# Weights of three head groups and of the last stage prepared block by block in the second layer, with their subtractions on VectorE

## The chip, the core and the metric

The kernel runs on one core of a Trainium2 chip. Its engines are TensorE (PE: matmuls, and weight loads, PEld), VectorE (DVE), ScalarE (ACT), GpSimd (POOL) and SyncE (SP), which issues most DMAs; 16 DMA engines carry these. The metric is the device time of one execution in microseconds; lower is better. Before the change it was 2925.16 us, the median of 3 runs (2920.04 to 2928.3).

## What is computed

One inference step of a two-layer hybrid decoder, on a prompt of 2048 positions and 8 samples of 4 positions, with a model width of 1024. Cut to its core:

```python
def gla_mixer(h, state0, norm_g, w_in, w_gate2, b_gate, out_norm_g, w_out):   # layer 0
    u = rmsnorm(h, norm_g)
    proj = u @ w_in
    q, k, v, gate, g_low = jnp.split(proj, ...)
    log_a = jax.nn.log_sigmoid((g_low @ w_gate2 + b_gate).astype(jnp.float32)) / A_GATE_NORMALIZER
    o, state = gla_recurrence(...)                 # 4 heads, a 128 x 512 state each
    o = rmsnorm(o, out_norm_g).reshape(bsz, seq_len, BRANCH_WIDTH).astype(h.dtype)
    return (o * jax.nn.silu(gate)) @ w_out, state

k, v = shared_kv(h, kv_norm, w_k, w_v, k_norm, pos)                           # once, after layer 0

q, gate = jnp.split(rmsnorm(h, norm_g) @ w_in, [BRANCH_WIDTH], axis=-1)       # layer 1
q = rope(rmsnorm(q.reshape(bsz, seq_len, B_HEADS, B_HEAD_DIM), q_norm_g), pos)
o = swa_banded(q, k, v, sinks)                     # 128 positions back, 32 query heads on 4 key heads
return (o.reshape(bsz, seq_len, BRANCH_WIDTH) * jax.nn.silu(gate)) @ w_out
```

## The kernel before

Every float32 operand of a matmul is split in two float16 tiles, a high and a low half (`split`: ScalarE writes the high half, VectorE the low one from it), and a product is three matmuls (`PASSES`). A weight must be split too. Weights of the second layer are split ahead of time by *preparations*: a load into `wraw` (3 buffers) on SP's queue, a `split` into `pst` (2 buffers), and a store on GpSimd's queue to memory, from which a later stage fetches the finished halves. There are two kinds:

- `Unit.prepare`: the weights of the second layer's projections, half a unit (128 x 512) at a time. Each of the 4 head groups (`gw[0]` to `gw[3]`) has 16 halves for `q` and the gate; group 0 has 8 more for keys and values.
- `form_steps`: the factors of the two output projections, which are computed with 7 products in place of 8. For each of 8 row blocks it forms 7 tiles of 128 x 512 from four quarters of the weight (`put`), three of them straight and four after a subtraction each (`sub`, on GpSimd). `wfa` is the first layer's output weight, `wfd` the second layer's.

Stages, with their time in the profile: the **first layer** (36 to 1195 us) runs over 4 heads, and in each over 4 *quarters* of the prompt (512 positions, `blocks`), with the next quarter's scores (`level_steps`) woven into this one's projections. In quarters 0, 1 and 2 `some(PR[j])` hands out preparations, 4, 8 and 7 of them at each of three places, at a lower priority (`behind(..., 200)`), so that they run later than they are written. The list has 192: 8 of the rope tables, 56 for `wfa`, 72 for the groups, 56 for `wfd`. Quarter 3 holds the samples' work, and quarters 2 and 3 also convert the next head's own weights into `W`. Then the **first output projection** (to about 1595 us).

The **second layer** (1595 to about 2600 us) runs over 64 *blocks*: 4 head groups times 16 chunks of 128 positions. The loop over `t` has three blocks in flight (n = t + 3): the matmuls of block n's projections (`f` in `ORDER`), the scores of block n - 2 (`A`) and the values of block n - 3 (`B`). `pin` holds TensorE to that written order. Scores go over VectorE (maximum), ScalarE (exponential, `o` and `lev`, L1432) and a `split` to `v`, from which SP's queue transposes them to `sth` and `pst` (L1438) for the values. `q` passes through `qT`, `kT`, `qe` and a transpose to `X` (L1389); keys and values go to memory as `Kd` and `Vd` and come back into `gl` and `rmask`. The next group's prepared weights are fetched in the group's 13th block. Last comes the second output projection (from about 2600 us), with `wfd` fetched from block 50 on.

The order on each engine is fixed when the program is built: a scheduler places instructions by priority, and an engine then runs them strictly in that order. Each DMA on SP's queue is also in order with all others there.

## Time and profile before

| | |
|---|---|
| median of 3 runs | 2925.16 us (2920.04 to 2928.3) |
| the profiled execution's own time | 2933.08 us |
| its span, first to last instruction | 2931.3 us |
| granted TensorE clock, mean | 0.974 |
| busy: matmuls, VectorE, ScalarE, GpSimd | 93%, 69%, 51%, 41% |

The profile is of one execution. It has instructions with their times, the idle time ahead of each and what ended it ("waits"), and busy times of any stretch. Names such as `pst<-wraw` are the program's tiles, output first; L197 is a line of the program. SPq and POOLq are the queues on which SP and GpSimd issue DMAs.

### The profile page before, as it was taken

Reading aid. Unit: us, or ns where it says so; the run is one execution under the profiler, and the core shown is the slowest. Engines: PE = TensorE matmul, PEld = TensorE weight load, DVE = VectorE, ACT = ScalarE, POOL = GpSimd, SP = SyncE. Lnnn points to the kernel's source line nnn. Section 1 sums busy time; section 2 is a strip of 40 time slices with the busy share of each in tenths; the row PEclk is TensorE's granted clock in tenths of the full one; section 3 lists DMA queues with packets and bytes.
Section 4 is the critical chain, followed back from the end, with each engine's and each line's share of the span. In section 5 each row is a group of like instructions: output and inputs, shape, how many; then the busy total and the mean of one; then the engine's idle time right before and its main releaser. Section 6 shows DMA issues by size and latency. Waiting matters only on the chain.

```text
span 2931.3 us, 52081 instructions
## 1 busy us (share of the span) xinstructions
PE 2727.8 (93%) x18942; PEld 1380.9 (47%) x18942; DVE 2034.1 (69%) x4055; ACT 1489.3 (51%) x3481; POOL 1199.9 (41%) x1591
## 2 busy tenths in 40 slices
PE   6889999899989989999998999999999999988999
PEld 3444544344434444444543555555555555543444
DVE  6778779778777888567572575677767766776653
ACT  6665666566556655433231555566666656651110
POOL 2254235422432355312123686566557656530000
PEclk9999999999999999999999999999999999999999
DMA  8353224453563354886559555867777778798651
GB/s 215 81 142 104 88 101 140 149 161 119 173 193 109 122 171 159 230 189 154 118 147 237 112 118 124 202 111 132 165 127 129 139 153 165 154 226 178 131 112 55
DMA packets 786202, 427.46 MB, mean 146 GB/s; under 512 B 630928, under 2 KB 700504, under 8 KB 785912
## 3 DMA queue, kind: packets, MB, share of 16 engines
q1 hardware_dynamic: 768504, 373.72, 55.7%
q0 software_dynamic: 15360, 50.34, 4.5%
q8 instruction: 148, 2.42, 0.4%
q14 instruction: 110, 0.90, 0.1%
q10 hardware_dynamic: 2080, 0.07, 0.0%
HBM read 153.58 MB, written 128.52 MB: 96 GB/s over the span
## 4 chain that ended last, share of the span: by engine, by line
PE 34%; DVE 10%; DMA 9%; ACT 8%; issue 5%; POOL 5%; SPq 3%; POOLq 0%; DVEq 0%; ACTq 0%
PE pj L100 16%; PE tr L100 9%; PE o L100 6%; PE kv L100 2%; ACT o L1432 2%; ACT v L197 1%; DMA pst<-v 1%; DVE v L198 1%; DMA wf<-pst 1%; DVE o L1427 1%; SPq L1668 1%; DVE lev L1427 1%; DVE pst L198 1%; DMA pre<-pst 1%; PE lev L100 1%
## 5 line engine op out<-in xcount | busy, mean ns | idle before, releaser
L100 PE MATMUL pj<-W,uT 128*128 128x512 f16 x5040 | 1205.2, 385 | 28.9 <-DVE sg L480 11.2
L100 PEld LDWEIGHTS <-uT 128*128 128x128 f16 x7072 | 653.5, 99 | 736.0 <-issue 72.1
L100 PE MATMUL tr<-W,uT 128*128 128x512 f16 x1536 | 367.2, 380 | 0.9 <-DVE gl L1065 0.9
L100 PEld LDWEIGHTS <-X 128*128 128x128 f16 x2840 | 193.9, 98 | 173.9 <-issue 23.5
L1432 ACT ACTIVATE o<-o,mx 128x256 f32<-128x256 f32 (+1 forms) x384 | 168.5, 439 | 165.7 <-DVE mx L1427 161.2
L186 POOL TENSOR_SCALAR rs_m<-ss 128x1 f32<-128x1 f32 (+3 forms) x190 | 52.5, 276 | 463.3 <-DVE ss L1329 211.0
L1427 DVE CUSTOM_DVE_ANT_0 o<-o,madd,nsink 128x256 f32<-128x256 f32 (+1 forms) x384 | 183.9, 479 | 51.6 <-PE o L100 47.4
L100 PE MATMUL pj<-uT,W 128*128 128x512 f16 (+1 forms) x912 | 185.7, 353 | 33.6 <-DMA uT<-ogT 24.9
L187 POOL TENSOR_TENSOR rs_r<-rs_m,mhalf 128x1 f32<-128x1 f32 (+3 forms) x186 | 193.3, 1040 | 13.8
L198 DVE SCALAR_TENSOR_TENSOR v<-o,v 128x512 f16<-128x512 f32 (+1 forms) x192 | 128.8, 671 | 97.9 <-ACT v L197 80.4
L100 PEld LDWEIGHTS <-W 128*128 128x128 f16 x2320 | 124.7, 99 | 133.4 <-issue 40.0
L100 PEld LDWEIGHTS <-sth 128*128 128x128 f16 x2176 | 120.5, 99 | 63.1 <-DMA sth<-v 12.0
L195 POOL TENSOR_TENSOR ogT<-og,ogT 128x512 f16<-128x512 f32 x68 | 88.0, 1294 | 141.2 <-ACT ogT L194 136.9
L510 POOL TENSOR_TENSOR E<-bt 128x256 f32<-128x256 f32 x96 | 72.1, 753 | 144.4 <-DVE X L195 89.8
L100 PE MATMUL o<-gl,X 128*128 128x256 f16 (+1 forms) x768 | 115.6, 274 | 7.4 <-DMA X<-qe 7.4
L197 ACT ACTIVATE v<-o 128x512 f16<-128x512 f32 (+1 forms) x192 | 111.3, 579 | 10.0 <-DMA sth<-v 6.5
L100 PEld LDWEIGHTS <-pst 128*128 128x128 f16 x1136 | 103.2, 99 | 26.9 <-DMA pst<-v 10.0
L100 PE MATMUL kv<-rmask,sth 128*128 128x64 f16 x1984 | 106.9, 194 | 9.3 <-DMA sth<-v 8.5
L100 PEld LDWEIGHTS <-qe 128*128 128x128 f16 x700 | 68.9, 99 | 91.3 <-issue 16.1
L195 DVE TENSOR_TENSOR X<-E,X 128x512 f16<-128x512 f32 x128 | 102.4, 800 | 13.7 <-ACT X L194 13.5
L100 PE MATMUL kv<-rmask,pst 128*128 128x64 f16 x992 | 102.1, 194 | 8.9 <-DMA pst<-v 8.9
L1432 ACT ACTIVATE lev<-lev,mx 128x256 f32<-128x256 f32 (+1 forms) x128 | 56.5, 441 | 102.1 <-DVE mx L1427 100.0
(531 smaller groups left out, 5465.2 us busy)
## 6 DMA issues: line engine op xcount, KB each, us to landing
pre<-pst POOLq DMA_DIRECT2D x72, 256.0 KB, 3.5
W<-pre SPq DMA_DIRECT2D x36, 512.0 KB
ogd<-ogT SPq DMA_DIRECT2D x68, 256.0 KB
wraw<-in_a_w_in_dram SPq DMA_DIRECT2D x64, 256.0 KB
wraw<-in_b_w_in_dram SPq DMA_DIRECT2D x64, 256.0 KB
oge<-ogT SPq DMA_DIRECT2D x64, 256.0 KB
wfa<-pst POOLq DMA_DIRECT2D x56, 256.0 KB, 3.2
wf<-pst POOLq DMA_DIRECT2D x56, 256.0 KB, 3.3
```

The lines of the kernel that those rows point to most:

```text
L100: return order(nc.tensor.matmul(*a, **k))
L186: pool.tensor_scalar(m[:n, :k], ss, a, b, ALU.mult, ALU.add)
L187: pool.tensor_tensor(r[:n, :k], m[:n, :k], mhalf[:n, :k], ALU.pow)
L195: eng.tensor_tensor(lo, src, hi, ALU.subtract)
L197: act(hi, src, AF.Copy, scale=sc)
L198: dve.scalar_tensor_tensor(lo, src, sc, hi, ALU.mult, ALU.subtract)
L510: pool.tensor_tensor(Ev[:, :, 0, :], ref, btv[:, :, 0, :], ALU.subtract)
L1427: dve.tensor_tensor_reduce(pm[:, z], pm[:, z], madd.rearrange("p a b -> p (a b)")[:, (2 - nk) * P :], -0.125, nsink[:, g * GRP + h : g * G ...
L1432: act(pm[:, z], pm[:, z], AF.Exp, scale=-1.0, bias=nm_[:, h : h + 1], accum_out=bx["sum"][:, h : h + 1])
L1668: nc.sync.dma_start(uT[j][:, :, hl, c * P : (c + 1) * P], ud[4 * j + c][:, hl], transpose=True)
```

## The change

The list of the first layer keeps 88 preparations: the rope tables, `wfa` and group 0; `PR` becomes 2, 4 and 2. Two new functions make the rest inside the second layer's loop, as a chain of 400 short steps (`asides`) at priority 60 behind their place:

- `unit_aside` for the 24 units of groups 1 to 3: two loads, then twice a conversion of 128 x 512 and its store, 6 steps.
- `forms_aside` for `wfd`, a quarter of the columns' width at a time (8 row blocks times 2): two loads of 128 x 2 x 256, then seven times a conversion of 128 x 256 and its store, 16 steps; the subtractions are on VectorE.

Both write to `og`, a tile with one buffer, and store from there on SP's queue; loads go to `wraw` as before. From block 1 on, `ASIDE` gives 14 steps to each block up to the 16th and 7 afterwards, between the groups of projection matmuls. `sub` in `form_steps` moves from GpSimd to VectorE for `wfa` too.

```diff
--- before.py
+++ after.py
@@ -53,7 +53,8 @@
 NV = 5
 KL = 5
 QL = 9
-PR = (4, 8, 7)
+PR = (2, 4, 2)
+ASIDE = (14, 7)
 
 
 class Ctx:
@@ -858,7 +859,7 @@
             nc.gpsimd.dma_start(fd[n][:, m], t)
 
         def sub(at, x, y):
-            pool.tensor_tensor(b[at], b[x], b[y], ALU.subtract)
+            dve.tensor_tensor(b[at], b[x], b[y], ALU.subtract)
 
         def s0():
             load("11", ku, 0)
@@ -923,10 +924,7 @@
     plan([lambda n=n, w=w, hf=hf: rope_table(n, w, hf) for n in range(2) for w in range(2) for hf in range(2)])
     for m in range(8):
         plan(form_steps(wfa, i["a_w_out"][0], m, m, m + 8, gs_o[:, m % 4 : m % 4 + 1]), True)
-    for w in gw:
-        plan(w.prepare())
-    for m in range(8):
-        plan(form_steps(wfd, i["b_w_out"][0], m, UP[m], UP[m] + 2, SWB), True)
+    plan(gw[0].prepare())
 
     hw = {0: head_weights(0)}
     cur = Blk(0, 0, hw[0])
@@ -1667,6 +1665,80 @@
         for hl in range(2):
             nc.sync.dma_start(uT[j][:, :, hl, c * P : (c + 1) * P], ud[4 * j + c][:, hl], transpose=True)
 
+    def unit_aside(u):
+
+        uniq[0] += 1
+        u.pre = dr.tile([P, 2, 1024], F16, tag=f"pre{uniq[0]}", name=f"pre{uniq[0]}")
+        src, t = u.parts[0][2], {}
+        nk = 512 // u.ncol
+
+        def load(half):
+            t["r", half] = T("wraw", [P, 512], F32, 3)
+            nc.sync.dma_start(t["r", half], src[half * P : (half + 1) * P])
+
+        def conv(half):
+            t[half] = T("og", [P, 2, 512], F16, 1)
+            k = u.kts[half]
+            split((t[half][:, 0], t[half][:, 1]), t["r", half], u.gs[:, k : k + 1])
+
+        def store(half):
+            nc.sync.dma_start(u.pre[:, :, half * 512 : half * 512 + 512], t[half])
+
+        return [lambda half=half: load(half) for half in range(2)], [lambda f=f, half=half: f(half) for half in range(2) for f in (conv, store)]
+
+    def forms_aside(m, q):
+
+        w, b = i["b_w_out"][0], {}
+
+        def load(r):
+            k = UP[m] + 2 * r
+            b[r] = T("wraw", [P, 2, 256], F32, 3)
+            nc.sync.dma_start(b[r], w[k * P : (k + 1) * P].rearrange("p (z c) -> p z c", z=2)[:, :, q * 256 : q * 256 + 256])
+
+        def open_():
+            g = T("og", [P, 512], F32, 1)
+            b["t"], b["o"] = g[:, :256], g[:, 256:].bitcast(F16).rearrange("p (z c) -> p z c", z=2)
+
+        def put(n, t):
+            split((b["o"][:, 0], b["o"][:, 1]), t, SWB)
+
+        def store(n):
+            nc.sync.dma_start(wfd[n][:, m, :, q * 256 : q * 256 + 256], b["o"])
+
+        sub = lambda d, x, y: dve.tensor_tensor(d, x, y, ALU.subtract)
+        b11, b12, b21, b22 = (lambda r=r, z=z: b[r][:, z] for r in range(2) for z in range(2))
+        todo = (
+            (0, lambda: open_(), b11),
+            (2, lambda: sub(b["t"], b12(), b11()), lambda: b["t"]),
+            (1, lambda: sub(b["t"], b22(), b["t"]), lambda: b["t"]),
+            (4, lambda: sub(b12(), b22(), b12()), b12),
+            (5, lambda: None, b22),
+            (3, lambda: None, b21),
+            (6, lambda: sub(b21(), b21(), b["t"]), b21),
+        )
+
+        def one(n, first, src):
+            first()
+            put(n, src())
+
+        out = []
+        for n, first, src in todo:
+            out += [lambda n=n, first=first, src=src: one(n, first, src), lambda n=n: store(n)]
+        return [lambda r=r: load(r) for r in range(2)], out
+
+    def chained(items):
+
+        out = list(items[0][0])
+        for n, (_, steps) in enumerate(items):
+            out += steps
+            if n + 1 < len(items):
+                out += items[n + 1][0]
+        return out
+
+    asides = [unit_aside(u) for w in gw[1:] for c_ in (w.q, w.g) for u in c_.units]
+    asides += [forms_aside(m, q) for m in range(8) for q in range(2)]
+    asides = behind(chained(asides), 60)
+
 
     end = pa[NCH // 2 - 1]
     fetch = {4: gw[0].kv[0].steps(), 0: [lambda c=c: u_load(0, c) for c in range(4)], 6: gw[0].q.steps(), 5: gw[0].g.steps()}
@@ -1836,13 +1908,17 @@
             "B": list(parts.pop(t)[1]) if t in parts else [],
         }
         nf = ORDER.count("f")
-        seen = done = 0
+        seen = done = past = 0
+        quota = ASIDE[n > NCH]
         for x in ORDER:
             if x == "f":
                 seen += 1
                 upto = len(fill) * seen // nf
                 run(fill[done:upto])
                 done = upto
+                while asides and n > 0 and past < seen * quota // nf:
+                    asides.pop(0)()
+                    past += 1
                 if trickle and seen % 3 == 0:
                     trickle.pop(0)()
                 if boundary and seen == 7 and n > TOT - NCH + 3:
@@ -1862,6 +1938,7 @@
                 pr = pairs[x // 2]
                 pr.l[x % 2] = [t_[:, 2 * x], t_[:, 2 * x + 1]]
                 pr.fetch(x % 2, pr.l[x % 2])
+        assert n < TOT - 16 or not asides
         if n in (TOT - 7, TOT - 3):
             run(quarters(wform_big, wfd, wf, {TOT - 7: 0, TOT - 3: 2}[n]))
         if n == TOT - 14:
```

What stands where, at three places (line numbers of the second program are its own). First, **ScalarE** in the first layer, in quarter 3 of head 1. `pst` rows are preparations; `E`, `X`, `sg`, `sth`, `og`, `v` are the layer's own work. Before:

```order
L197 ACTIVATE pst_5918<-wraw_5905,gso 128x512
L197 ACTIVATE pst_5927<-wraw_5603,gso 128x512
L512 ACTIVATE E_5878<-E_5878 128x512
L512 ACTIVATE E_6047<-E_6047 128x512
L194 ACTIVATE X_5884<-E_5878 128x512
L479 ACTIVATE sg_5949<-pj_5873 128x512
L197 ACTIVATE pst_5935<-wraw_5915,gso 128x512
L197 ACTIVATE sth_6020<-st_6003 128x512
L197 ACTIVATE pst_5945<-wraw_5943,gso 128x512
```

and with the change:

```order
L198 ACTIVATE v_5608<-pj_5555 128x512
L513 ACTIVATE E_5823<-E_5823 128x512
L195 ACTIVATE X_5665<-E_5659 128x512
L513 ACTIVATE E_5850<-E_5850 128x512
L480 ACTIVATE sg_5720<-pj_5627 128x512
L198 ACTIVATE sth_5792<-st_5771 128x512
L614 ACTIVATE og_5799,ss_5800<-o_5777 128x512
L195 ACTIVATE X_5829<-E_5823 128x512
L195 ACTIVATE ogT_5810<-og_5799 128x512
```

The preparations are gone there; over whole quarters, ScalarE's rows that convert from `wraw` go from 12, 22 and 33 in quarters 1 to 3 of head 1 to 9, 27 and 4, from 11, 25 and 33 in head 2 to 11, 25 and 4, and from 12, 20 and 24 in head 3 to 9, 15 and 0.

Second, **ScalarE** in the second layer, in the first block of group 1 (block 16). `o`, `lev` are exponentials of scores, `v` their high half, `ogT` the result of an earlier block. Before:

```order
L197 ACTIVATE v_20699<-o_20701 128x512
L1432 ACTIVATE o_20768,sm_3514_20698<-o_20768,mx_20697 128x256
L1328 ACTIVATE E_20790<-pj_20712 128x512
L1432 ACTIVATE o_20768,sm_3514_20698<-o_20768,mx_20697 128x256
L197 ACTIVATE v_20699<-o_20768 128x512
L1432 ACTIVATE lev_20816,sm_3514_20698<-lev_20816,mx_20697 128x256 x2
L197 ACTIVATE v_20814<-lev_20816 128x512
L1432 ACTIVATE o_20833,sm_3514_20698<-o_20833,mx_20697 128x256 x2
L194 ACTIVATE ogT_20876<-wraw_20874 128x512
```

and with the change, where `og<-wraw` and `og<-og` are the new conversions:

```order
L198 ACTIVATE v_20521<-o_20523 128x512
L198 ACTIVATE og_19920<-wraw_19907 128x256 x3
L195 ACTIVATE ogT_20474<-wraw_20472 128x512
L198 ACTIVATE og_20296<-wraw_20210 128x256
L198 ACTIVATE og_20296<-og_20296 128x256
L1430 ACTIVATE o_20594,sm_3433_20520<-o_20594,mx_20519 128x256 x2
L1326 ACTIVATE E_20619<-pj_20534 128x512
L198 ACTIVATE v_20521<-o_20594 128x512
L198 ACTIVATE og_20296<-og_20296 128x256
L1430 ACTIVATE lev_20646,sm_3433_20520<-lev_20646,mx_20519 128x256 x2
L198 ACTIVATE og_20296<-wraw_20210 128x256
L198 ACTIVATE v_20644<-lev_20646 128x512
```

Five conversions now stand between two exponentials that followed each other but for one high half; each of the five waits for the store of the one ahead of it, since `og` has one buffer. Over blocks 3 to 41 there are mostly 3 to 5 in a block, with 7 in block 13, 8 in block 16 and 7 in block 17.

Third, **SP's queue** at the same place, from a block's transpose to `X` on; `wf<-og` rows are the new stores. Before:

```order
L1389 DMA_TRANSPOSE X_20668<-qe_20665 128x8x128
L1438 DMA_TRANSPOSE sth_20779<-v_20699 128x8x128
L1438 DMA_TRANSPOSE pst_20781<-v_20700 128x8x128
L1375 DMA_TRANSPOSE gl_16124<-Kd_16092 128x2x128
L1373 DMA rmask_16089<-Vd_16108 128x128
L1375 DMA_TRANSPOSE gl_16124<-Kd_16093 128x2x128
L1341 DMA bt_21178<-rtd 128x128
L1438 DMA_TRANSPOSE sth_20844<-v_20814 128x8x128
```

and with the change:

```order
L1387 DMA_TRANSPOSE X_20486<-qe_20483 128x8x128
L1706 DMA wf_134<-og_19920 128x2x256
L1706 DMA wf_132<-og_19920 128x2x256
L1706 DMA wf_135<-og_19920 128x2x256
L1706 DMA wf_129<-og_20296 128x2x256
L632 DMA oge_126<-ogT_20474 512x1x256
L1696 DMA wraw_20545<-in_b_w_out_dram 128x2x256
L1706 DMA wf_131<-og_20296 128x2x256
L1436 DMA_TRANSPOSE sth_20605<-v_20521 128x8x128
L1706 DMA wf_130<-og_20296 128x2x256
L1436 DMA_TRANSPOSE pst_20607<-v_20522 128x8x128
```

Six stores and a load have moved in between the transposes; those to `sth` and `pst`, which followed `X` directly, come after five of the stores.

## The prediction

> **What bounds the kernel now.** The first view is the busy time by stage; each row has the stretch in us, its length, then busy us (and instructions) of matmuls, weight loads, VectorE, ScalarE and GpSimd, the granted clock, the DMA engines' share and GB/s.
>
> ```profile
> span 2931.3 us, 52081 instructions
> ...
> 36.40:1195.00 1158.60, 1053.13 (x6555) 501.95 (x6553) 903.35 (x1540) 696.51 (x1293) 449.14 (x609) 0.97 0.46 139
> 1610.00:1816.60 206.60, 206.24 (x1614) 111.60 (x1612) 127.50 (x325) 113.38 (x333) 149.12 (x210) 1.00 0.57 120
> 1816.60:1909.30 92.70, 88.50 (x706) 47.87 (x703) 56.30 (x151) 49.65 (x143) 55.88 (x77) 0.96 0.73 177
> 1909.30:2274.10 364.80, 357.34 (x3255) 204.18 (x3254) 262.22 (x690) 232.76 (x711) 233.81 (x295) 0.99 0.71 133
> ```
>
> TensorE bounds both layers, unequally. In the first layer (36 to 1195 us) it idles 105.5 us of 1158.6. In the second, between 1610 and 1816.6 us it idles 0.4 us of 206.6, and 11.7 us in the 457.5 us after that. So work that leaves the first layer can give back up to a hundred microseconds, and in the second layer there is nothing to win and all of it to lose. The waits say who ends TensorE's idle time in the first layer, and what VectorE and ScalarE stood in front of (total us, times, longest):
>
> ```profile
> PE kv L100 <- ACT v L197: 20.5, 12, 4.2
> PE pj L100 <- DVE sg L480: 20.2, 14, 3.7
> ...
> DVE pst L198 <- ACT pst L197: 88.7, 73, 3.8
> ...
> ACT pst L197 <- POOL wraw L861: 31.0, 15, 4.1
> ACT pst L197 <- DMA pre<-pst: 25.6, 19, 4.2
> ```
>
> TensorE waits for `v` and `sg`, which ScalarE and VectorE make; those two stand at `pst`, the conversions of weights. The same stretch cut into quarters of a head shows that this costs. First whole rows (quarters 0 to 3 of head 1, then 2 and 3 of heads 2 and 3), then the instructions on `wraw` alone in head 1: VectorE, ScalarE, GpSimd, with counts.
>
> ```profile
> 307.90:370.60 62.70, 59.90 (x360) 28.57 (x359) 45.77 (x85) 39.20 (x72) 15.85 (x23) 1.00 0.31 93
> 370.60:448.60 78.00, 74.61 (x424) 35.20 (x424) 64.34 (x118) 46.11 (x91) 28.92 (x39) 0.98 0.32 110
> 448.60:528.60 80.00, 69.63 (x393) 32.21 (x391) 66.87 (x91) 45.62 (x78) 43.28 (x53) 0.98 0.42 134
> 528.60:613.60 85.00, 71.78 (x528) 34.93 (x527) 68.34 (x108) 50.99 (x97) 37.60 (x52) 0.94 0.55 167
> 747.30:824.80 77.50, 66.92 (x383) 30.98 (x382) 59.31 (x94) 46.20 (x80) 30.49 (x43) 1.00 0.55 181
> 824.80:909.20 84.40, 71.77 (x524) 35.35 (x523) 63.47 (x109) 50.89 (x97) 32.81 (x45) 0.94 0.58 184
> 1049.00:1120.20 71.20, 64.68 (x367) 29.78 (x366) 61.46 (x88) 42.95 (x77) 42.66 (x50) 0.98 0.51 166
> 1120.20:1195.00 74.80, 66.06 (x499) 31.93 (x497) 56.82 (x92) 39.12 (x75) 39.96 (x50) 0.93 0.55 167
> ...
> 307.90:370.60 62.70, 9.67 (x12) 8.37 (x12) 1.26 (x1) 1.00 0.31 93
> 370.60:448.60 78.00, 9.28 (x11) 8.31 (x12) 8.00 (x6) 0.98 0.32 110
> 448.60:528.60 80.00, 19.28 (x22) 15.30 (x23) 15.55 (x12) 0.98 0.42 134
> 528.60:613.60 85.00, 23.05 (x34) 21.53 (x34) 6.71 (x5) 0.94 0.55 167
> ```
>
> TensorE's idle time is the length less the first busy figure: 2.8, 3.4, 10.4 and 13.2 us in head 1, with 12, 12, 23 and 34 conversions on ScalarE. Up to 12 cost little, above that about half a microsecond each.
>
> **The first layer: minus 37 us.** By the order of instructions, ScalarE's conversions (preparations and the next head's own) become 9, 11 and 9 in quarter 1 of heads 1 to 3, 27, 25 and 15 in quarter 2, and 4, 4 and 0 in quarter 3. So the work doesn't leave quarter 2; quarter 3 is emptied. Quarters 2 and 3 idle now 10.4 + 13.2 + 10.6 + 12.6 + 6.5 + 8.7 = 62.0 us. I price 27, 25 and 15 conversions by the rows at 11, 10.5 and 5 us, and quarter 3 at 2.5 us each: 34 us, a gain of 28. Quarter 1 gives 1. Head 0 loses 14 preparations; at 28 us for the 84 that leave the other quarters that is 5. The rest is the subtractions:
>
> ```profile
> L861 POOL TENSOR_TENSOR wraw<-wraw,wraw 128x512 f32<-128x512 f32 x61 | 82.9, 1365 | 39.3 <-DMA wraw<-in_a_w_out_dram 15.1 <-DMA wraw<-in_b_w_out_dram 10.5 <-DVE pst L198 7.2
> ...
> L493 DVE TENSOR_TENSOR E<-qT,kT 128x512 f32<-128x512 f32 x14 | 10.2, 725 | 11.0 <-ACT kT L432 10.8
> ```
>
> The 32 that stay in this layer move from GpSimd (1.37 us each) to VectorE, whose nearest row is 0.73 us: 23 us more on VectorE against 104 halves of some 0.8 us that leave it, and ScalarE's 31 us of waiting on GpSimd go. I count 3 us. Together 37; from 15 (quarter 2 gets worse, as it takes more conversions than now) to 55 (all six quarters fall to 2.5).
>
> **The second layer: plus 60 us.** Here the change adds 48 conversions of 512 columns and 112 of 256, 64 subtractions, 80 loads and 160 stores. Engine time is not the price: per block at most 4.67 conversions, or some 3.4 us on ScalarE and 3.9 on VectorE, beside 10.3 and 11.6 us of 18.8. GpSimd's queue loses 104 stores; SP's gains 9.3 issues a block of some 0.5 us (as `Vd`'s below), which alone would fit too. The price is that all 160 results pass through **one buffer**, `og`, and that loads and stores stand on SP's queue among the transposes of the attention. A conversion can't begin until the store of the one before has landed. So one round trip follows another: ScalarE half, VectorE half, store, landing. Its parts:
>
> ```profile
> L197 ACT ACTIVATE pst<-wraw,gsb 128x512 f16<-128x512 f32 x64 | 45.7, 717 | 48.1 <-DMA pre<-pst 21.4 <-issue 10.1 <-DVE og L616 4.0
> L197 ACT ACTIVATE W<-wraw,gsa 128x256 f16<-128x256 f32 x24 | 10.7, 497 | 4.7 <-DMA wraw<-in_a_w_in_dram 4.0 <-DVE ogT L198 0.8
> ...
> L198 DVE SCALAR_TENSOR_TENSOR pst<-wraw,gsb,pst 128x512 f16<-128x512 f32 x64 | 53.4, 836 | 31.6 <-ACT pst L197 31.5
> L198 DVE SCALAR_TENSOR_TENSOR w<-tr,w 128x256 f16<-128x256 f32 x14 | 5.8, 414 | 0.0
> ...
> 1704.62 0.52 SPq L1369 DMA_DIRECT2D Kd<-lvm  x1
> 1706.90 1.17 SPq L1375 DMA_TRANSPOSE gl<-Kd  x1
> 1715.70 0.41 DVE L198 SCALAR_TENSOR_TENSOR w<-tr,w 128x256 f16<-128x256 f32 x1
> 1716.84 0.53 SPq L1354 DMA_DIRECT2D Vd<-w  x1
> 1718.81 0.32 SPq L1373 DMA_DIRECT2D rmask<-Vd  x1
> ...
> pre<-pst POOLq DMA_DIRECT2D x72, 256.0 KB, 3.5
> wf<-pst POOLq DMA_DIRECT2D x56, 256.0 KB, 3.3
> ```
>
> The trace has no store of `og` to a prepared weight, so I bound its landing. `gl<-Kd` starts once the 256 KB of `Kd` are there, 2.28 us after their issue; for the 128 KB of `Vd` it is 1.97 us. From GpSimd's queue the same 256 KB took 3.5 and 3.3 us. I take the middle, 2.9 and 2.65 us, because the engines will carry much more than they did around 1704, and 0.25 us of queueing on SP and VectorE (the `w` half ended at 1716.11 and its store was issued 0.73 us later; other stores went at once). A 512-column trip is then 0.72 + 0.84 + 2.9 + 0.25 = 4.7 us (from 3.84 to 5.3), a 256-column one 0.5 + 0.45 + 2.65 + 0.25 = 3.85 us (from 2.9 to 4.5). How many a block must hold, and how long blocks are, by one VectorE write of `qT` in each (the first and last row begin and end on such a write, so these are 11, 5 and 25 blocks):
>
> ```profile
> 1610.00:1816.60 206.60, 0.00 (x0) 0.00 (x0) 7.55 (x12) 0.00 (x0) 29.07 (x33) 1.00 0.57 120
> 1816.60:1909.30 92.70, 0.00 (x0) 0.00 (x0) 3.41 (x5) 0.00 (x0) 13.23 (x15) 0.96 0.73 177
> 1909.30:2274.10 364.80, 0.00 (x0) 0.00 (x0) 17.31 (x26) 0.00 (x0) 66.99 (x75) 0.99 0.71 133
> ```
>
> A block lasts 18.8 us, then 18.5, then 14.6. Units give 144 steps, three to a conversion, 14 to a block: 10.3 blocks with 4.67 trips, 21.9 us for 18.8, plus 3.1 each or **32 us**. The 80 form steps left in the first group, 16 to 7 conversions, give 5.7 blocks (of 18.5 us) with 6.1 trips, 23.5 us, plus 5.0 each or **28 us**. From block 17 on, 7 steps make 3.06 trips, 11.8 us of 14.6: they fit, at nothing. The ends are 0 (3.84 and 2.9 us fit: 17.9 and 17.8) and 62 + 51 = 113 us. The wait is not ScalarE's alone: behind a held conversion stand the exponentials of the next scores, behind a held store on SP the transposes of those scores.
>
> The Trainium skill, DMA: Bandwidth & Descriptors, section "Anatomy of one DMA — SWDGE (gpsimd) path", gives a DMA a fixed cost of about 2.0 us plus its bytes over 436 GB/s, an estimate of 2.6 us for 256 KB and 2.3 for 128 KB. The trace's 2.28 and 1.97 us lie 0.3 below that and its 3.5 above; that most of it is fixed, which speaks against short steps, agrees. By that rule the two terms would be 19 and 17 us and the sum about nothing, as in the case "even" below.
>
> **The sum.** 60 less 37 is 23 us slower. The profiled execution took 2933.1 us, 1.8 around its span, and would take 2956; the median of the runs shown, 2925.2 us, lies 8 us below it, which gives **2948 us**.
>
> **Rivals.**
> - *The trips hide: faster.* Landing stays at `Kd`'s and `Vd`'s 2.28 and 1.97 us: trips of 4.1 and 3.2 us make 19.1 and 19.4 us blocks, plus 3 and 5 us, and 37 less 8 gives 2896. For it: SP and ScalarE idle much, and blocks have run 206 us without a stall. Against: those two landings were measured at a DMA share of 0.57. It decides where a unit trip stays below 4.3 us. Chance 0.27.
> - *Even.* Landing a quarter of the way from `Kd` and `Vd` to GpSimd's stores, 2.6 and 2.3 us: 35 us lost, 37 won, 2923. Chance 0.14.
> - *The DMA engines fill: much slower.* Units bring 2.4 MB to a block, 127 GB/s on top of 120. Between the first and fourth quarter rows 74 GB/s cost 0.24 of the engines, so the share goes from 0.57 to 0.98. With 4.0 us to land a unit trip is 5.8 us, plus 8.3 us a block, 86; with the forms' upper 51 and less 37, 100: 3025. Against: the share of 0.73 at 1816 came with 4 us of idle time only. Chance 0.08.
> - *The first layer gives little*, as quarter 2 keeps its conversions: 15 instead of 37, 2970. Chance 0.10.
>
> **The numbers.** The forecast itself, 10 to 55 us slower, has 0.41. Below 2894 lies under half of the first rival, 0.11, above 2995 the filled engines and a little of the forecast, 0.09, so the range is 2894 to 2995. A measurement can tell some 0.3%, 9 us, from no change: faster 0.27, same 0.14, slower 0.59.
>
> **What would show it.** Right: TensorE idle in the first layer near 70 us, with quarter 3 near 2.5; blocks 1 to 16 at 21 to 24 us; ScalarE's waits on stores of `og` well over 100 us in all, and SP's on VectorE's `og`. Wrong: blocks of 19 us with TensorE idle under 10 us up to block 16 (the trips fit), stores of `og` landing in 2.3 us, or a loss after block 17, where I count none.

## The result, and the profile after

The changed kernel takes **3031.09 us** (median of 4 runs, 3023.55 to 3032.74) against 2923.14 us (4 runs) of the kernel before beside it: a ratio of 1.0362, 95% interval 1.0338 to 1.0387. It is slower by 108 us; the prediction was 2948 us, within 2894 to 2995. The direction was right, the size was not. Times are medians of a kernel's executions; one execution in experiment 3, the engine work alone, took 10412.84 us for a reason that is not known, and that kernel's interval is without it (its median is 2896.6 without it, 2897.6 with it).

The first view is again the busy time by stage: stretch, length, busy us and instructions of matmuls, weight loads, VectorE, ScalarE and GpSimd, granted clock, DMA share, GB/s. The rows are the first layer, the first output projection, blocks 1 to 11, 12 to 16, 17 to 41 and 42 to 63 of the second layer, and the last projection.

```profile
span 3030.9 us, 52181 instructions
...
37.10:1133.00 1095.90, 1030.27 (x6541) 496.23 (x6539) 817.20 (x1475) 639.89 (x1193) 302.44 (x449) 0.99 0.37 106
1133.00:1533.90 400.90, 378.42 (x2027) 175.26 (x2024) 238.68 (x381) 120.61 (x246) 83.75 (x97) 0.97 0.73 172
1551.50:1813.00 261.50, 229.06 (x1674) 119.95 (x1674) 156.51 (x371) 136.71 (x376) 153.66 (x210) 0.94 0.74 180
1813.00:1934.60 121.60, 87.77 (x675) 47.98 (x676) 76.06 (x194) 58.23 (x170) 57.83 (x77) 0.86 0.71 180
1934.60:2374.80 440.20, 373.19 (x3189) 208.13 (x3187) 320.54 (x811) 259.96 (x790) 243.46 (x295) 0.91 0.70 147
2374.80:2698.00 323.20, 308.40 (x2825) 175.71 (x2823) 230.82 (x607) 201.32 (x608) 194.87 (x248) 0.99 0.80 161
2698.00:3030.90 332.90, 314.42 (x1802) 148.78 (x1800) 190.56 (x323) 55.44 (x114) 7.34 (x9) 0.96 0.61 132
```

Set beside the same stages of before: the first layer went from 1158.6 to 1095.9 us, a gain of **63** (TensorE's idle time from 105.5 to 65.6, its busy time from 1053.1 to 1030.3 at a clock of 0.99 in place of 0.97). Blocks 1 to 11 went from 206.6 to 261.5, 12 to 16 from 92.7 to 121.6, and 17 to 41, where the prediction counted no loss, from 364.8 to 440.2: **159** lost in all. That is 96 on balance; the two profiled executions lie 99.6 us apart. DMA engines stand at 0.70 to 0.74 of full use there, and not at their limit.

In quarters of a head (2 and 3 of head 1, then of head 2) the first layer shows what was forecast for it: quarter 3 is empty of preparations and idles 1.3 and 0.6 us, quarter 2 idles 6.4 and 7.6.

```profile
436.40:506.80 70.40, 63.95 (x362) 29.28 (x360) 61.87 (x107) 45.18 (x82) 24.92 (x38) 0.98 0.45 145
506.80:577.30 70.50, 69.21 (x541) 35.14 (x542) 46.43 (x81) 35.07 (x68) 16.75 (x24) 1.00 0.15 44
723.80:793.90 70.10, 62.46 (x352) 28.43 (x351) 61.84 (x102) 43.34 (x79) 24.13 (x37) 0.95 0.46 147
793.90:863.50 69.60, 69.00 (x541) 35.02 (x540) 46.01 (x80) 35.09 (x68) 16.20 (x23) 1.00 0.12 35
```

The waits of the second layer (us in total, times, longest; the first two rows from blocks 1 to 11, the others from blocks 17 to 41) name the chain through `og`: ScalarE stands in front of a store that has not landed, VectorE behind ScalarE, SP behind VectorE, and TensorE in the end in front of `v`, which the same two engines make.

```profile
ACT og L198 <- DMA pre<-og: 49.5, 25, 6.6
DVE og L199 <- ACT og L198: 60.6, 33, 4.7
...
ACT og L198 <- DMA wf<-og: 79.4, 49, 5.4
DVE og L199 <- ACT og L198: 57.6, 38, 4.1
PE lev L104 <- DVE v L199: 22.1, 4, 7.0
PE kv L101 <- DVE wraw L1472: 19.9, 4, 10.5
SPq L1706 <- DVE og L199: 43.9, 27, 4.0
```

Two trips, instruction by instruction, in the timeline of a later block (start, duration, engine, line; in brackets the idle time before and what ended it):

```profile
2042.85 0.42 ACT L198 ACTIVATE og<-wraw 128x256 f16<-128x256 f32 x1 [3.51 <-DMA wf<-og]
2045.64 0.42 ACT L198 ACTIVATE og<-wraw 128x256 f16<-128x256 f32 x1 [0.35 <-DMA wf<-og]
...
2043.30 0.43 DVE L199 SCALAR_TENSOR_TENSOR og<-wraw,og 128x256 f16<-128x256 f32 x1 [2.04 <-ACT og L198]
2046.33 0.42 DVE L199 SCALAR_TENSOR_TENSOR og<-wraw,og 128x256 f16<-128x256 f32 x1
...
2043.76 0.37 SPq L1706 DMA_DIRECT2D wf<-og  x1
2045.32 1.23 SPq L1436 DMA_TRANSPOSE sth<-v  x1
2046.65 1.27 SPq L1436 DMA_TRANSPOSE pst<-v  x1
2048.02 1.22 SPq L1373 DMA_TRANSPOSE gl<-Kd  x1
2049.33 0.53 SPq L1371 DMA_DIRECT2D rmask<-Vd  x1
2049.95 1.04 SPq L1706 DMA_DIRECT2D wf<-og  x1
```

The first store was issued as soon as VectorE was done (43.73 to 43.76). The second result was ready at 2046.75 and its store went out at 2049.95: it stood 3.2 us behind two transposes and a load. That is the term that the prediction put at 0.25 us.

Followed so over 150 of the 160 trips (landing: from a store's issue to its last semaphore event), the parts are, in us. The other ten, all of units, ran ahead of block 1, from 1451.6 us on, where the prediction had none.

| | ScalarE and VectorE, with the wait between | wait for SP's queue | landing, mean (median) | until the next conversion | trip | predicted |
|---|---|---|---|---|---|---|
| units, blocks 1 to 11 (38 trips) | 1.69 | 0.80 | 2.98 (2.69) | 0.76 | 6.24 | 4.7 |
| factors, first group (31) | 1.00 | 0.97 | 2.51 (2.06) | 0.15 | 4.68 | 3.85 |
| factors, later (81) | 1.29 | 1.37 | 2.44 (2.19) | 0.30 | 5.35 | 3.85 |

A trip runs from one conversion to the next, so 81 of 5.35 us fill blocks 17 to 41 by definition (433 of 440 us). That the trips set the pace is read from the gap from a landing to the next conversion: its median is 0.08 us in each row, so mostly the next conversion was already standing there.

### The profile page after: what moved, and what is told of

Same layout as the page of the kernel before. It is cut to its first block, busy times and chain, and to the rows that moved or that the text cites. A ratio compares the mean times of both kernels' runs of the same rounds, so it can differ in the third digit from the quotient of the medians.

```text
span 3030.9 us, 52181 instructions
## 1 busy us (share of the span) xinstructions
PE 2748.5 (91%) x18942; PEld 1391.3 (46%) x18942; DVE 2056.0 (68%) x4207; ACT 1495.8 (49%) x3537; POOL 1062.8 (35%) x1423
## 5 line engine op out<-in xcount | busy, mean ns | idle before, releaser
L101 PE MATMUL tr<-W,uT 128*128 128x512 f16 x1536 | 374.6, 386 | 3.8 <-DVE st L1056 3.0
L101 PEld LDWEIGHTS <-sth 128*128 128x128 f16 x2176 | 121.9, 99 | 99.6 <-issue 42.8
L196 DVE TENSOR_TENSOR X<-E,X 128x512 f16<-128x512 f32 x128 | 98.3, 768 | 10.5 <-ACT X L195 10.0
L195 ACT ACTIVATE X<-E 128x512 f16<-128x512 f32 x128 | 79.5, 621 | 46.8 <-PE lev L101 22.6
```

The source lines that it names most:

```text
L101: return order(nc.tensor.matmul(*a, **k))
L195: act(hi, src, AF.Copy)
L196: eng.tensor_tensor(lo, src, hi, ALU.subtract)
```

## The experiments

They start from the changed kernel unless it is said otherwise. Runs that leave preparations out read weights that were made once for group 0 and for the first layer.

**1. Is it the one buffer, or SP's queue?** Four edits. Two buffers (`st` is free in most of the second layer); stores from GpSimd's queue; both; and the subtractions back on GpSimd.

```diff
-            t[half] = T("og", [P, 2, 512], F16, 1)
+            t[half] = T("st", [P, 2, 512], F16, 2)
...
-            b["t"], b["o"] = g[:, :256], g[:, 256:].bitcast(F16).rearrange("p (z c) -> p z c", z=2)
+            b["t"] = T("og", [P, 256], F32, 1)
...
+            b["o"] = T("st", [P, 2, 256], F16, 2)
             split((b["o"][:, 0], b["o"][:, 1]), t, SWB)
```

> The prepared pieces are written to a second tile name with two buffers, so two pieces can be on their way at once. Theory A (one buffer makes the trips serial, and held conversions and stores block three queues): a trip of 6.24 us (units), 4.68 and 5.35 us (forms) is shared by two pieces, 4.67 x 3.1 = 15 us, 6.1 x 2.4 = 14 us and 3.06 x 2.7 = 8 us a block, below the 18.8, 18.5 and 14.6 us that the blocks took before; the second layer's +159 us falls to 0 to 60, ScalarE's waits on stores fall from 175 to under 50 us, and the time is 2860 to 2920 us, likeliest 2885. Theory B (the added work of the engines itself, or the DMA engines, is what costs): the second layer keeps 120 to 160 us, 2990 to 3030 us. Theory C (SyncE's queue, where stores wait behind transposed loads, is what costs, whatever the buffers): half goes, 2940 to 2970 us.

```diff
-            nc.sync.dma_start(wfd[n][:, m, :, q * 256 : q * 256 + 256], b["o"])
+            nc.gpsimd.dma_start(wfd[n][:, m, :, q * 256 : q * 256 + 256], b["o"])
```

> Still one buffer; the prepared pieces are stored from GpSimd's queue, not from SyncE's. Theory A (serial trips) with the 0.8 to 1.37 us in SyncE's queue as its mis-sized part: trips of 5.5, 3.9 and 4.0 us, blocks of 4.67 x 5.5 = 26, 6.1 x 3.9 = 24 and 3.06 x 4.0 = 12 us; blocks 17 to 41 lose under 20 us in place of 75, blocks 1 to 16 lose 60 to 80: 2930 to 2960 us. If GpSimd's own queue or a longer landing (3.3 to 3.5 us on it in the kernel before) takes the place of SyncE's queue: trips as long as now, 3010 to 3050 us. Theory B (engine work): no change, 3020 to 3040.

> Both: two buffers, and stores from GpSimd's queue. Theory A: little beyond two buffers alone, 2860 to 2910 us. Theory C (SyncE's queue): clearly less than two buffers alone, by 30 us or more. Theory B: 2990 to 3030 us.

```diff
-        sub = lambda d, x, y: dve.tensor_tensor(d, x, y, ALU.subtract)
+        sub = lambda d, x, y: pool.tensor_tensor(d, x, y, ALU.subtract)
```

> The subtractions go back to GpSimd in both layers; all else as in the changed kernel. Theory A: the subtractions are not what costs; the chain through the buffer keeps its length but for the subtraction ahead of 4 of 7 conversions, 3015 to 3055 us, and the first layer keeps its 60 us within 10. Rival D (the second part of the change, subtractions on a VectorE that is busy to 75% of the first layer, costs the time): 2960 to 3000 us.

| run | median, us | ratio to before, 95% interval | blocks 1-11 | 12-16 | 17-41 |
|---|---|---|---|---|---|
| the changed kernel | 3031.1 | 1.0338 to 1.0387 | 261.5 | 121.6 | 440.2 |
| two buffers | 2968.3 | 1.0137 to 1.0180 | 255.6 | 103.1 | 410.4 |
| GpSimd's queue | 3077.7 | 1.0502 to 1.0550 | 288.0 | 139.1 | 451.0 |
| both | 2967.3 | 1.0130 to 1.0174 | 257.1 | 106.8 | 407.9 |
| subtractions on GpSimd | 3001.3 | 1.0256 to 1.0296 | 259.0 | 122.4 | 422.8 |

The second buffer takes 63 us off, so the serial trips are part of the cause; but 48 us over the kernel before are left where 2860 to 2920 was expected, and blocks 1 to 11 hardly moved. Theory A as it stood falls. The time lies in theory C's range, but C falls too: with two buffers, storing from GpSimd's queue changed nothing (2967.3). A third buffer was not tried. GpSimd's queue is worse by 47 us with one buffer. Its waits in the second layer point to why: a store on that queue waits for VectorE at GpSimd's own head, and behind it stands what GpSimd makes for the block; TensorE then stood 132.5 us until VectorE had read the last output out of `kv` (L1472), where the changed kernel has 1.9, 31.3 and 19.9 in its three stretches. The time, 3077.7 us, lies above every forecast.

```profile
PE kv L101 <- DVE wraw L1472: 132.5, 20, 17.7
...
POOL wf L1706 <- DVE og L199: 99.9, 64, 5.5
POOL pre L1685 <- DVE og L199: 60.8, 22, 9.4
```

The subtractions' return gave 30 us back, 12 of them before block 0 (at 1521.8 us in place of 1533.9) and 17 in blocks 17 to 41: more than expected of theory A, and at the edge of rival D. The 12 are not shown to be theirs: the other kernels of experiments 1 to 3, all but one with subtractions on VectorE, begin block 0 anywhere from 1520.4 to 1534.4 us.

**2. With two buffers, is it late raw pieces, or the pace?**

```diff
-            out += steps
-            if n + 1 < len(items):
-                out += items[n + 1][0]
+            nxt = list(items[n + 1][0]) if n + 1 < len(items) else []
+            cut = 2 if len(steps) == 4 else 8
+            out += steps[:cut] + nxt[:1] + steps[cut:] + nxt[1:]
...
-ASIDE = (14, 7)
+ASIDE = (9, 9)
```

> Two buffers, and the raw piece of the next conversion loaded two to six steps ahead in place of right ahead of it; as many steps in a block as before. Theory L (with two buffers, conversions at the head of ScalarE's queue wait for raw pieces that were asked for too late: 37.9 us in blocks 1 to 11 and 17.3 us later): blocks 1 to 11 fall from 255 to 215 to 235 us, the time from 2968 to 2925 to 2945 us. Theory P (14 steps a block are more than what PE covers, whatever they wait for): blocks 1 to 11 stay at 245 to 255 us, 2955 to 2970 us.

> Two buffers, and the steps of preparation at one pace: 9 a block all along, in place of 14 and then 7. Theory P (only what goes over the cover of a block costs): with 3 to 4 trips a block blocks 1 to 16 lose 10 to 25 us in place of 59, blocks 17 to 44 lose at most 10 more than now: 2920 to 2945 us. Theory W (each trip costs the same wherever it stands, since its work on ScalarE and VectorE is itself what PE waits for): no change, 2955 to 2975 us. Theory L: a part, 2940 to 2955.

> Both: early loads and 9 steps a block, with two buffers. By P and L together the waits that are left are those of the conversions' own work: 2890 to 2925 us. By W: 2945 to 2975.

> The same with the subtractions on GpSimd, as they were before the change. If a subtraction costs by its place on VectorE, where PE waits for the splits behind it (with one buffer the move back gave 30 us, 12 of them in the first layer): 15 to 30 us less than with VectorE. If its gain was only that of a shorter chain through the one buffer: within 12 us, the first layer's alone.

Early loads gave 2973.3 us (1.0163 to 1.0206), the even pace 2989.2 (1.0217 to 1.0263), both 2991.1 (1.0204 to 1.0263), with subtractions on GpSimd 2983.4 (1.0191 to 1.0243). P's forecast for the even pace failed, and even W's was 14 us too low: blocks 1 to 16 took 353.8 us in place of 358.5 and blocks 17 to 47 523.4 in place of 493.8, so the first 16 blocks lost 54 us with 9 steps each and 59 with 14, and those up to 47 lost 74 with 9 and 44 with 7. A step costs no less where there are fewer of them; as the kinds of step in those blocks differ too, no more is shown. Of L the run says nothing, because the edit did not do what it was for: the wait for raw pieces in blocks 1 to 11 was 37.9 us with two buffers and is 33.4 with loads written earlier.

```profile
ACT st L198 <- DMA wraw<-in_b_w_in_dram: 37.9, 18, 5.5
```

```profile
ACT st L198 <- DMA wraw<-in_b_w_in_dram: 33.4, 20, 4.7
```

The subtractions' place was worth 8 us by the medians here, with intervals that overlap, and block 0 began no sooner (1531.5 us against 1528.7). That the larger gain of the first run came with the shorter chain through one buffer fits this, but is not shown.

**3. The price of the preparation, in parts.** Four kernels: without any preparation in the second layer; with its engine work alone; with its DMA steps alone; and two buffers with loads and stores both on GpSimd's queue.

```diff
-    asides = [unit_aside(u) for w in gw[1:] for c_ in (w.q, w.g) for u in c_.units]
-    asides += [forms_aside(m, q) for m in range(8) for q in range(2)]
-    asides = behind(chained(asides), 60)
+    for w in gw[1:]:
+        for a_, b_ in ((w.q, gw[0].q), (w.g, gw[0].g)):
+            for u, v in zip(a_.units, b_.units):
+                u.pre = v.pre
+    wfd = wfa
+    asides = []
```

> The preparation in the second layer is left out altogether (groups 1 to 3 read the prepared weights of group 0, the output stage the factors of the first layer, so the output is another; PE's work, loads and all else are as in the changed kernel). This prices what the first layer gained and what the whole of the preparation costs. All theories: the second layer as before the change, 993 us for its 63 blocks, first layer as in the changed kernel: 2923 - 62 = 2861 us, 2850 to 2875.

```diff
-            t["r", half] = T("wraw", [P, 512], F32, 3)
-            nc.sync.dma_start(t["r", half], src[half * P : (half + 1) * P])
+            t["r", half] = idf.unsqueeze(1).to_broadcast([P, 4, P])
...
-            nc.sync.dma_start(u.pre[:, :, half * 512 : half * 512 + 512], t[half])
+            pass
```

> Only the engine work of the preparation: conversions and subtractions as many and as wide, of a resident tile into two buffers, with no load and no store (weights read as in the run without preparation, so the output is another). Theory W (each conversion costs by its own time on ScalarE and VectorE, which are in order and stand ahead of PE's releasers): 2920 to 2960 us, most of what two buffers left (2968). Theory Q (the DMA steps on SyncE's queue, and conversions held by landings, are what costs): 2860 to 2885 us.

```diff
-            split((t[half][:, 0], t[half][:, 1]), t["r", half], u.gs[:, k : k + 1])
+            pass
...
-            nc.sync.dma_start(u.pre[:, :, half * 512 : half * 512 + 512], t[half])
+            nc.sync.dma_start(own[:, :, half * 256 : half * 256 + 256], t["r", half].rearrange("p (z c) -> p z c", z=2))
```

> Only the DMA steps: raw pieces loaded, and stored again as they are, in as many loads and stores of the same bytes on SyncE's queue, with no conversion and no subtraction (weights read as in the run without preparation, so the output is another). Theory Q: 2920 to 2960 us. Theory W: 2860 to 2885 us. If both this and the engine work alone are cheap, the cost is in their coupling: a conversion held at the head of a queue by a landing.

```diff
-            nc.sync.dma_start(t["r", half], src[half * P : (half + 1) * P])
+            nc.gpsimd.dma_start(t["r", half], src[half * P : (half + 1) * P])
```

> Two buffers, and both loads and stores of the preparation on GpSimd's queue; SyncE's queue holds what it held without them. Theory Q (SyncE's queue): 2890 to 2930 us. Theory W: 2955 to 2980 us, as with two buffers alone (2968).

| run | median, us | ratio to before, 95% interval | second layer, blocks 0-62 | TensorE idle there | SP issuing there |
|---|---|---|---|---|---|
| the kernel before | 2921.3 | | 992.4 | 26.5 | 715 |
| no preparation | 2859.1 | 0.9753 to 0.9811 | 988.3 | 26.5 | 714 |
| engine work alone | 2897.6 | 0.9891 to 0.9925 | 1031.7 | 59.7 | 712 |
| DMA steps alone | 2920.1 | 0.9976 to 1.0002 | 1041.7 | 65.9 | 840 |
| all of it, two buffers | 2968.3 | 1.0137 to 1.0180 | 1098.2 | 107.9 | 837 |
| all of it, one buffer | 3031.1 | 1.0338 to 1.0387 | 1151.2 | 150.3 | 834 |
| two buffers, all DMA steps on GpSimd's queue | 3022.2 | 1.0297 to 1.0421 | 1143.9 | 144.1 | 735 |

This is the account. Neither theory's range holds throughout: the engine work lay between the two, the DMA steps at the lower end of Q's, all DMA steps on GpSimd's queue above both. Without the preparation the kernel takes 2859 us, which confirms the first layer's gain of 62. Above that the engine work costs 39 us by itself, the DMA steps 61, both together with two buffers 109 (so about 10 for their coupling), and the single buffer another 63: **172 us** in all, for 62 won. The prediction had the first two at nothing. In the profiled executions 14 us of the DMA steps' price lie ahead of block 0 (1534.4 us in place of 1520.4), where 28 of the 240 ran, and 53 in the second layer. Another reservation: with nothing to wait for, the scheduler bunches the conversions of the work-alone run more than the others (VectorE busy 200 us in blocks 1 to 11, against 163 with two buffers).

What the engine work does by itself is seen in TensorE's waits for `v`: 35.8 us in blocks 0 to 62, against 6.7 without preparation. What the DMA steps do by themselves is seen on SP's queue. Around the transpose to `X`, in block 4 without preparation, then in block 5 with the DMA steps alone:

```profile
1599.01 1.26 SPq L1387 DMA_TRANSPOSE X<-qe  x1
1601.49 0.33 SPq L1352 DMA_DIRECT2D Vd<-w  x1
1603.20 0.32 SPq L1371 DMA_DIRECT2D rmask<-Vd  x1
1604.36 1.23 SPq L1436 DMA_TRANSPOSE sth<-v  x1
```

```profile
1644.68 1.45 SPq L1687 DMA_DIRECT2D pre<-wraw  x2
1646.17 0.63 SPq L1354 DMA_DIRECT2D Vd<-w  x1
1647.61 0.51 SPq L1687 DMA_DIRECT2D pre<-wraw  x1
1648.17 1.39 SPq L1389 DMA_TRANSPOSE X<-qe  x1
1649.60 0.58 SPq L1373 DMA_DIRECT2D rmask<-Vd  x1
1650.30 1.23 SPq L1438 DMA_TRANSPOSE sth<-v  x1
```

The gaps that let a transpose go out as soon as its operand was there are filled. Over all 64 blocks, the mean time from the end of VectorE's write of `qe` to the issue of its transpose is 1.2 us without preparation and 3.5 with the DMA steps alone; the transposes land in 3.8 us in both. TensorE's waits for transposes up to 2350 us, first without preparation, then with the DMA steps alone:

```profile
PE o L101 <- DMA X<-qe: 4.0, 2, 3.2
...
PE kv L101 <- DMA sth<-v: 3.6, 3, 1.5
PE kv L101 <- DMA pst<-v: 2.8, 4, 0.9
```

```profile
PE o L101 <- DMA X<-qe: 17.4, 8, 4.8
...
PE kv L101 <- DMA pst<-v: 8.8, 9, 1.2
PE kv L101 <- DMA sth<-v: 7.7, 7, 3.9
```

These are 24 of the 39 us that TensorE idles more. In the kernels that also convert, they are not where TensorE stands: `qe` waits 1.4 us for its transpose's issue in the changed kernel and 1.2 with two buffers, and TensorE waits 1.3 and 2.3 us for `X`. With two buffers it stands at `v`, from VectorE:

```profile
PE o L101 <- DVE v L199: 40.2, 22, 5.5
```

So 39, 61 and 10 are prices of separate kernels, not parts seen in one; by which way the DMA steps cost in the whole kernel is not shown.

With all DMA steps on GpSimd's queue SP issues as before (735 us), and yet TensorE waits 102.7 us for `X` in blocks 0 to 41, 27 times. There the transposes were issued 1.3 us after `qe` and landed in 4.2 us (3.8 without preparation), so it is mainly `qe` that came late. GpSimd, which has a part in it, stood 82 us at the new stores; that this made it late is likely, but not shown.

**4. Bytes or steps? And is there a better place?** The DMA steps alone were cut to a quarter of their columns, or to the loads; and the same preparation was moved to the stage between the layers, in part and whole, with subtractions on GpSimd. (The whole keeps `PR` at 2, 4 and 2 and hands out 22 steps a pair.)

```diff
-            nc.sync.dma_start(t["r", half], src[half * P : (half + 1) * P])
+            nc.sync.dma_start(t["r", half][:, :128], src[half * P : (half + 1) * P, :128])
```

> As the run with the DMA steps alone (2920 us), with as many loads and stores, each of a quarter of the bytes (the output is that of the run without preparation). If the bytes cost (DMA engines, or transposed loads that land later behind them): 2870 to 2885 us, a quarter to a third of the 61 us. If the steps on SyncE's queue cost, by their number: 2905 to 2925 us.

> Of the DMA steps only the 80 loads, 21 of some 48 MB, on SyncE's queue; no store, no conversion (the output is that of the run without preparation). By bytes: 61 x 21/48 = 27 us, 2880 to 2893. By number of steps (80 of 240): 20 us, 2875 to 2883. If it is the stores' waits on the queue that cost: 2860 to 2872.

```diff
-PR = (2, 4, 2)
+PR = (3, 6, 5)
...
+    for m in range(8):
+        plan(form_steps(wfd, i["b_w_out"][0], m, UP[m], UP[m] + 2, SWB), True)
+    for w in gw[1:]:
+        plan(w.prepare())
...
-        weave([f for n in range(2, 7) for f in pa[p_].steps(n)], ld + rest + mix(sm[:6], some(4) if p_ > 1 else []))
+        weave([f for n in range(2, 7) for f in pa[p_].steps(n)], ld + rest + mix(sm[:6], some(10) if p_ > 1 else []))
```

> The units of groups 1 to 3 are prepared in the stage between the layers (up to 10 steps in each of five pairs, with two buffers and stores from GpSimd's queue, as the first layer does it), the last stage's factors in the first layer as before the change, nothing in the second layer, subtractions on GpSimd. If the loss belongs to the second layer's blocks: the first layer gains about half of its 62 us, the stage between the layers loses 0 to 20: 2885 to 2920 us. If PE pays for this work wherever it stands: 2920 to 2945.

> The same with the last stage's factors too in the stage between the layers, up to 22 steps a pair. The first layer gains its 62 us and more; 104 steps in 280 us put about 110 us of work on a VectorE that has 240 of 400 us there, and about 48 MB on DMA engines that are at 0.73: the stage loses 20 to 80 us, 2880 to 2940 us.

A quarter of the bytes still costs 50 of the 61 us: 2909.3 (0.9926 to 0.9969). Blocks 1 to 11, first with all bytes, then with a quarter: the DMA share falls from 0.77 to 0.60, near the 0.55 without preparation, and TensorE's idle time stays (16.7 and 16.1 us).

```profile
1548.70:1779.80 231.10, 214.42 (x1628) 114.02 (x1629) 124.59 (x325) 112.98 (x333) 148.76 (x211) 0.97 0.77 188
```

```profile
1548.70:1775.40 226.70, 210.58 (x1615) 112.83 (x1616) 126.97 (x325) 113.14 (x333) 148.88 (x210) 0.98 0.60 127
```

So it is mostly the steps, not the bytes. The 80 loads alone cost 17 us (2875.7, 0.9808 to 0.9868), near their third of 240 steps; but in the profiled execution 11 of these lie ahead of block 0 (at 1531.8 us), and the second layer is 9 us longer, of 53, so that there a store costs more than a load. The Trainium skill, DMA: Bandwidth & Descriptors, section "Issuing engines are not separate DMA queues", says that another issuing engine saves only the sequencer's time to initiate a DMA, "which is usually small relative to the DMA itself". Small it is here too, 0.6 us a step (126 us for the 212 in the table's stretch, against landings of 2.4 to 3.0 us in the changed kernel); but on a queue that TensorE's transposes pass through, the steps were the larger part of these 61 us.

The stage between the layers is no better place: 2951.1 us with 34 of the 48 unit halves there (1.0066 to 1.0126; the other 14 were still handed out in the first layer), 2974.9 with all (1.0137 to 1.0205), both above every forecast. With the part, quarter 3 of head 3 began at 1131.2 us (1120.2 before the change, 1068.5 in the changed kernel): a third of the 104 moved preparations left the first layer and nothing was won there, for a reason that is not known; from there to block 0 it took 483 us in place of 475. With all of it that quarter began at 1068.2, and the time from there to block 0 grew from 465 to 545 us; 19 of the stores went out after it, and blocks 1 to 11 took 234 us in place of 207. No run with the whole preparation beat the kernel before.

**5. The second part of the change alone**, in the kernel before:

```diff
-            pool.tensor_tensor(b[at], b[x], b[y], ALU.subtract)
+            dve.tensor_tensor(b[at], b[x], b[y], ALU.subtract)
```

> The kernel before, with only the second part of the change: the subtractions of both sets of factors, all in the first layer, on VectorE in place of GpSimd. If a subtraction costs by its place on VectorE: the changed kernel lost about 12 us in the first layer for one set, so 15 to 25 us for two, 2935 to 2948 us. If it does not: 2915 to 2927.

It gave 2929.8 us, a ratio of 1.0016 (1.0002 to 1.0031), between the two expectations: a few microseconds slower. The second part is not what made the change slow.

## Why the prediction was right in direction and wrong in size

- **First layer, minus 37: right in mechanism, too small.** 63 lies above its own bounds, 15 to 55. 40 us came from idle time, as counted. Quarter 3 came out at 1.3 and 0.6 us against 2.5 assumed, quarter 2 of heads 1 and 2 at 6.4 and 7.6 against 11 and 10.5. Another 23 us are TensorE's busy time, which shrank with a higher granted clock; the prediction had no term for it. The run without preparation gives 62.
- **Landing, 2.9 and 2.65 us: right.** Measured 2.98 and 2.44 to 2.51.
- **"0.25 us of queueing on SP and VectorE": the term that failed in the trip.** It was taken from one store that waited while "other stores went at once", in a queue that did not yet carry the change's steps. Measured: 0.80 to 1.37 us on SP's queue alone, and 0.15 to 0.76 us until the next conversion runs. The two engines took 1.29 us in the later blocks against 0.95 counted.
- **Units plus 32, factors in group 0 plus 28:** 55 in blocks 1 to 11 and 29 in blocks 12 to 16, although ten of the 48 unit conversions had run ahead of block 1.
- **"From block 17 on ... they fit, at nothing": wrong, 75 us, the largest error of the sum.** 81 trips ran in these 25 blocks, 3.24 in each; at 5.35 us in place of 3.85 they take 17.3 us, and a block had lasted 14.6. Two buffers, with which a trip need not end before the next begins, still left 46 us there. That part is not the serial trip alone; as ScalarE still waited 35.6 us for stores in it, it is not all the steps themselves either.
- **"Engine time is not the price" and SP's issues "alone would fit too": the step behind most of the error.** It compared busy sums with the block's length, and left out when the work comes: what stands in a queue ahead of TensorE's next operand delays it, however much idle time the queue has. The parts alone cost 39 and 61 us.
- **The rival of full DMA engines, 3025 us,** came near the time by luck, from another cause: the share was 0.70 to 0.74, and three quarters of the bytes were worth 11 us.
- The signs named beforehand: quarter 3 and ScalarE's waits on stores of `og` (49.5 and 79.4 us in two rows above) came as written; blocks 1 to 11 took 23.8 us each and 12 to 16 24.3, where 21 to 24 was named; and the loss after block 17 was the sign named for "wrong".

## What to carry to other kernels

A step that is put into a stage bounded by one engine is not free because the other engines' busy shares leave room: in-order queues make it stand in front of that engine's operands, and here, each in a kernel of its own, 240 DMA steps of 0.6 us on the queue of the transposes cost 61 us, and conversions on ScalarE and VectorE 39. Count what stands behind each added instruction in its queue, and take the wait for that queue from the order after the change, not from a single wait of before. A buffer that is written, stored and written again needs two copies before its place is judged; then ask whether the work is cheaper where it was.

## What the runs showed of the hardware

The granted clock followed TensorE's idle time within the same blocks 1 to 11. Without preparation it was 1.00 with 0.2 us idle; the rows with two buffers and with stores on GpSimd's queue, one kernel each, show 0.95 with 30.9 us and 0.88 with 64.5 us.

```profile
1534.70:1741.20 206.50, 206.31 (x1608) 111.70 (x1609) 127.41 (x323) 113.09 (x333) 148.97 (x210) 1.00 0.55 120
```

```profile
1548.50:1804.00 255.50, 224.62 (x1666) 119.15 (x1664) 163.41 (x384) 142.00 (x386) 154.86 (x210) 0.95 0.79 193
```

```profile
1545.10:1833.10 288.00, 223.53 (x1629) 119.11 (x1630) 162.06 (x368) 139.50 (x376) 183.36 (x254) 0.88 0.70 165
```

TensorE's busy time for one recorded matmul grew as the clock fell: 206.31 us over 1608 are 0.128 us, and the other two rows give 0.135 and 0.137. So a stall costs more than its own length; in the first layer the reverse gave 23 us. The Trainium skill, TensorE: Matmul & The Clock Gate, section "What's actually happening", states that an idle window of about 3.4 us puts the clock to half and a busy one restores it; the traces agree: in these three stretches TensorE idled for over 3.4 us at a time 0, 3 and 8 times, and their clock records have 0.5 for 0, 27.3 and 68.3 us in all, in pieces of 3.4 to 17.1 us, and 1.0 otherwise. No run here separates the price of the clock from that of the stall.

A subtraction of 128 x 256 on VectorE took 0.41 to 1.82 us (least, median, greatest below, in ns), without a cause that the runs isolate.

```profile
L1708 DVE TENSOR_TENSOR og<-wraw x16: 415/426/1529, 1791.7 to 2331.2; 128x256 f32<-128x256 f32 x16
L1708 DVE TENSOR_TENSOR wraw<-wraw,wraw x16: 408/425/1821, 1793.0 to 2333.5; 128x256 f32<-128x256 f32 x16
```
